# Two-layer hybrid block on one core: expert outputs combined on chip in layer 2, keys as logs in the recurrence

## The chip, the cores and the metric

The kernel runs on one core of a Trainium2 chip. The metric is the device time of one execution in microseconds (us), as the median of several runs. The engines are named as in the profile: PE (TensorE, with PEld for its weight loads), DVE (VectorE), ACT (ScalarE), POOL (GpSimd) and SP (SyncE, which here only issues transfers).

## What is computed

The block has two layers. Each modulates 512 tokens (256 of context, 256 latent) of width 1024, projects them once, runs three token mixers side by side, merges them, and then sends each token through two of 32 experts. The second layer's context is not needed after the mixers, so its mixture of experts sees 256 tokens only.

```python
for layer in range(2):
    hl = xl * (1 + sc1_l) + sh1_l                     # the same for the context tokens
    p = split(hl @ w_in[layer])
    ya, yb, yc = gdn_mixer(p), window_attention_mixer(p), hgrn_mixer(p)
    xl = layer_norm(ALPHA * xl + g1_l * branch_merge(ya, yb, yc, ...))
    h2 = xl * (1 + sc2_l) + sh2_l
    y = hierarchical_moe(h2, ...)                     # top group, two experts in it
    xl = layer_norm(ALPHA * xl + g2_l * y)

# hgrn_mixer: per channel, both directions, chunks of 64
logf = log(max(lb + (1 - lb) * sigmoid(x), 1e-30))
k = (1 - lb) * sigmoid(-x)
b = cumsum(logf)                                      # within the chunk
a[t, s] = sum_d q[t, d] * k[s, d] * exp(b[t, d] - b[s, d])      # s <= t
o = (q * exp(b)) @ S + a @ v
S = exp(b_last) * S + (k * exp(b_last - b)).T @ v

# one expert
hid = silu(xb @ w1[e]) * (xb @ w3[e]);  y = hid @ w2[e]
```

## The kernel before, in words

`backbone` writes both layers out as straight code; a planner orders the instructions of each engine by priority, and `fill` and `bg` set pieces of projection and of modulation work by hand between the steps of the mixers. A conditional block is a unit that nothing is moved across. All transfers of weights are issued by SP in the order written.

**Start.** `mod_prepare` (L215) makes the modulation's inputs, `mod_steps` (L263) multiplies them with the columns of one modulation vector in pieces of 512 KB (L281), and L294 to L303 turn the result into columns. The vectors 0 and 1 come first, then the tokens X are loaded; L424 to L434 transpose X, apply scale and shift (ACT, L432) and split the result into a high and a low part of type fp32r (L433, L434), 256 tokens at a time.

**Projections.** `split_unit` (L140) loads a raw piece of 1024 columns' worth, rounds it to the high part on ACT (L152) and takes the low part on POOL or DVE (L154); `mm3` (L202 to L204) multiplies in three passes. The 17 calls of `init_rows` (background work of the first layer) write X into the two regions of the table `ysD`, so that rows that no expert writes hold numbers.

**HGRN2 (C).** `forget_gates` (L929) makes `kf` (the keys) and `lf` on ACT, POOL and DVE, with L945 the addition of the lower bound in the second layer and L946 the floor; `log_gates` (L948) takes the log of `lf`, 128 channels of both directions at a time (L953). `head_begin` (L1065) makes for each of four heads the cumulative sums `bc` by matmul, the transposed keys `kt` (a copy on ACT), and the decayed keys (`es`, sums at L1087, the product on POOL at L1090). `level_decays` (L1118) subtracts boundary sums into `E` on DVE and takes Exp on ACT; `level_products` (L1137) multiplies the left half of `E` by `kt` on DVE (L1147, two instructions per level and head) and the right half by the queries on POOL, and PE multiplies the two.

**Router (R).** L1481 and L1483 pick the experts on DVE. `permute(q)` (L1542) sorts tokens into expert order by matmul with selection matrices, and copies the sorted rows to `XS` on DVE and ACT. Ahead of `permute(0)` POOL scales a row of norm weights (L1562) and applies scale and shift to X (L1566, 1024 wide, two instructions per block of 128 tokens). Then the token weights are scattered to `wsD` by POOL.

**Experts (E).** `expert_steps` (L1613) computes a block of up to 64 tokens: `weights` loads `wc` from `wsD`, `rows` copies the block's rows (L1634), `up` multiplies with w1 or w3 (L1640, PE in 128 by 64 column tiles, two tiles at a time), `gate` (L1644), `turn` (two transposes and the copy L1651), `down` (L1659, column tiles again), L1663 the weighting, and L1670 two stores of 128 KB to `ysD`. The loop (L1740 to L1765) writes the steps of expert e and e+1 into each other: the first `up` of e+1 stands around `turn` of e, then `down` of e, then the second `up` of e+1. An expert with over 64 tokens runs a conditional block more. An expert's weights are 6 MB in six pieces; the ring of slots holds 18 MB in this loop (15 and `NE2` = 3 slots of 1 MB).

**End.** Four indirect loads gather the rows of `ysD` (L1776), four additions put them to X (L1780), `normalise` ends with L377, then scale, shift and the store of the output.

Of the kernel before, what the change touches and what calls it, by code (L numbers as in the profile page):

```python
# [20 lines left out]
P = 128  # L21
# [60 lines left out]
def backbone(ctx: ExitStack, tc: tile.TileContext, a, out, dbg=None, upto=None):  # L82
# [55 lines left out]
    BOTH = (nc.gpsimd, nc.vector)  # L138

    def split_unit(kt, pieces, engines=(nc.gpsimd,)):  # L140

        n = sum(cn for p in pieces for _, cn in p)
        hr, lr = [wtile(x)[:, :kt * n].bitcast(F32R).rearrange("p (k c) -> p k c", k=kt) for x in ("whi", "wlo")]
        off = 0
        for piece in pieces:
            pn = sum(cn for _, cn in piece)
            rv = rtile()[:, :kt * pn].rearrange("p (k c) -> p k c", k=kt)
            o = 0
            for load, cn in piece:
                load(rv[:, :, o:o + cn])  # L150
                o += cn
# [13 lines left out]
    def cols_unit(src, c0, n, kt=KD, engines=(nc.gpsimd,)):  # L165
        w = 1024 // kt
        return split_unit(kt, [[col_load(src, c, min(w, c0 + n - c))] for c in range(c0, c0 + n, w)], engines)
# [46 lines left out]
    def mod_prepare():  # L214
        with tc.tile_pool(name="modp", bufs=1) as pool:  # L215
            r = pool.tile([2 * NLAYER * KD, P], F32, name="lnr")
            for i, n in enumerate(("ln2_g", "ln2_b")):
                nc.sync.dma_start(r[i * NLAYER * KD:(i + 1) * NLAYER * KD], a[n].rearrange("l (k p) -> (l k) p", p=P))
# [5 lines left out]
            for i, n in enumerate(("ln1_g", "ln1_b")):  # L224
                nc.sync.dma_start(r[2 * NLAYER * i:2 * NLAYER * (i + 1)], a[n].rearrange("l (h c) -> (l h) c", c=512))
            for i in range(NLAYER):
                nc.sync.dma_start(r[4 * NLAYER + 4 * i:4 * NLAYER + 4 * i + 4],
# [21 lines left out]
            for i in range(NLAYER):  # L249
                b = pool.tile([6 * KD, P], F32, name="bm", tag="bm")  # L250
                nc.sync.dma_start(b, a["b_mod"][i].rearrange("(v p) -> v p", p=P))
# [7 lines left out]
                for v in (1, 4):  # L259
                    nc.vector.tensor_scalar(bmT[i][:, v], bmT[i][:, v], 1.0, None, op0=OP.add)  # L260

    def mod_steps(l, v, ahead=0):
# [29 lines left out]
        def finish():  # L292
# [6 lines left out]
            ps = ps_tile([P, 2, P])  # L299
            for x in range(2):  # L300
                transpose(ps[:, x], row[:, x * P:(x + 1) * P])
            for s in range(2):
                nc.vector.tensor_add(modT[l][:, v, s].rearrange("p (j x) -> p x j", x=2),  # L303
                                     ps.rearrange("p x (j m) -> p x j m", m=32)[:, :, :, s],
                                     bmT[l][:, v].rearrange("p (j x) -> p x j", x=2))
# [56 lines left out]
    def normalise(bs):  # L362
# [13 lines left out]
        for i, b in enumerate(bs):  # L376
            nc.vector.tensor_scalar(X[:, b], X[:, b], r[:, i:i + 1], nm[:, i:i + 1], op0=OP.mult, op1=OP.add)  # L377
# [4 lines left out]


    mod_prepare()
    for v in (0, 1):
        for f in mod_steps(0, v):
            f()
# [1426 lines left out]
```

## Time and profile before

| | us |
|---|---|
| median of 3 runs | 2718.26 |
| the three runs | 2717.43, 2718.26, 2724.83 |
| the profiled execution | 2724.99 |
| its span, first to last instruction | 2723.5 |
| PE busy | 2202.1 (81%) |
| DVE busy | 1257.1 (46%) |
| POOL busy | 713.6 (26%) |
| ACT busy | 615.9 (23%) |
| read from and written to HBM | 592.36 and 59.03 MB |
| mean granted clock of PE | 0.907 |

The profiled execution is one program run recorded by the hardware. The shares are means over stages with different limits: a share tells nothing until it is read for one stage. The page cuts the span into 40 equal slices of 68 us; in each, a digit is the busy share of an engine in tenths, and a number the rate at which the transfers moved bytes. From there the stages are read one by one, with windows of the trace (busy time per engine in a stretch), the waits of one engine, and timelines (start, duration, engine, line, operation, and in brackets the idle time before it with what ended that).

### The profile page before, as it was taken

To read this page: it belongs to the slowest core of one execution; us is meant where nothing else is said; L and a number is where in the kernel's file an instruction comes from. 1 tells how busy PE (TensorE), PEld (TensorE's weight loads), DVE (VectorE), ACT (ScalarE), POOL (GpSimd) and SP (SyncE) were. 2 spreads that over 40 slices of the span, in tenths; PEclk is the share of its full clock that TensorE was granted. 3 is DMA by queue.
4 is the path that set the end of the run, shared out by engine and by line. 5 is a ranking of instruction groups with operands and counts; after the bars stand their busy time and mean duration, and the time that the engine had idled before them with its cause. 6 is when DMAs were issued, how large, how long until landed. Compare 5 with 4: busy or idle time off the path is not lost. (4 is left out here: it accounts for less than half of the span.)

```text
span 2723.5 us, 42854 instructions
## 1 busy us (share of the span) xinstructions
PE 2202.1 (81%) x16239; PEld 1554.5 (57%) x16239; DVE 1257.1 (46%) x2596; ACT 615.9 (23%) x1233; POOL 713.6 (26%) x757
## 2 busy tenths in 40 slices
PE   7998988887988889877773899986787669778774
PEld 3665985676776554444441666875777545344432
DVE  4749545787448322212224779457875411111112
ACT  2421335543332000000000342335543200000000
POOL 1242220454244211111112242213554131111111
PEclk9999999898989899888987899988998889998897
DMA  9466351222657469999997258342356949999995
GB/s 319 146 204 201 117 186 47 76 86 89 197 174 248 155 244 361 416 416 416 417 411 247 64 167 258 107 161 62 102 147 191 333 173 383 417 416 417 417 416 217
DMA packets 325669, 655.09 MB, mean 241 GB/s; under 512 B 48662, under 2 KB 228414, under 8 KB 282136
## 3 DMA queue, kind: packets, MB, share of 16 engines
q1 hardware_dynamic: 291058, 600.76, 60.9%
q10 hardware_dynamic: 21382, 26.79, 2.8%
q0 software_dynamic: 12960, 23.94, 2.6%
q8 instruction: 171, 2.80, 0.4%
q14 instruction: 98, 0.80, 0.1%
HBM read 592.36 MB, written 59.03 MB: 239 GB/s over the span
## 5 line engine op out<-in xcount | busy, mean ns | idle before, releaser
L1640 PE MATMUL ps<-we,xt 128*64 128x256 f32 x4224 | 548.4, 412 | 180.3 <-DMA we<-in_w 161.1
L1640 PEld LDWEIGHTS ps<-we,xt 128*64 128x64 f32 x4224 | 330.6, 148 | 389.1 <-issue 262.7
L154 POOL TENSOR_TENSOR wlo<-raw,whi 128x1024 fp32r<-128x1024 f32 (+1 forms) x84 | 206.9, 2464 | 548.7 <-ACT whi L152 508.5
L202 PE MATMUL ps<-hT,whi 128*128 128x512 f32 (+2 forms) x880 | 328.0, 373 | 2.0 <-ACT whi L152 1.9
L204 PE MATMUL ps<-hT,wlo 128*128 128x512 f32 (+2 forms) x880 | 317.9, 361 | 0.3 <-DVE wlo L154 0.3
L203 PE MATMUL ps<-hT,whi 128*128 128x512 f32 (+2 forms) x880 | 317.6, 361 | 0.0
L1659 PE MATMUL ps<-we,hd 128*64 128x512 f32 x1104 | 251.8, 598 | 4.7 <-DVE hd L1651 4.7
L1670 POOL DMA_DIRECT2D ysD<-yo x134 | 71.4, 533 | 698.1 <-DMA ysD<-yo 348.2
L1644 ACT ACTIVATE hd<-ps 128x256 f32<-128x256 f32 x69 | 26.4, 383 | 969.0 <-PE ps L1640 969.0
L152 ACT ACTIVATE whi<-raw 128x1024 fp32r<-128x1024 f32 x174 | 180.0, 1044 | 236.0 <-PE ps L203 130.3
L1663 DVE SCALAR_TENSOR_TENSOR yo<-ps,wc,g 128x512 f32<-128x512 f32 x69 | 51.8, 751 | 374.5 <-PE ps L1659 337.0
L202 PEld LDWEIGHTS ps<-hT,whi 128*128 128x128 f32 (+1 forms) x880 | 172.9, 196 | 43.0 <-issue 13.4
L204 PEld LDWEIGHTS ps<-hT,wlo 128*128 128x128 f32 (+1 forms) x880 | 172.4, 196 | 31.2 <-issue 6.9
L203 PEld LDWEIGHTS ps<-hT,whi 128*128 128x128 f32 (+1 forms) x880 | 173.0, 197 | 25.2 <-issue 3.7
L1651 DVE COPY hd<-ps 128x256 f32<-128x256 f32 x69 | 29.3, 425 | 305.2 <-PE ps L110 305.1
L154 DVE TENSOR_TENSOR wlo<-raw,whi 128x1024 fp32r<-128x1024 f32 x90 | 147.3, 1638 | 45.2 <-ACT whi L152 39.4
L1659 PEld LDWEIGHTS ps<-we,hd 128*64 128x64 f32 x1104 | 78.7, 138 | 135.9 <-issue 120.0
L1627 POOL DMA_DIRECT2D wc<-wsD x138 | 71.7, 520 | 173.2 <-DMA ysD<-yo 71.3
L203 PE MATMUL ps<-wlo,hT 128*128 128x256 f32 x384 | 109.8, 286 | 1.6 <-DVE wlo L154 1.6
L202 PE MATMUL ps<-whi,hT 128*128 128x256 f32 x384 | 110.5, 288 | 0.0
L204 PE MATMUL ps<-whi,hT 128*128 128x256 f32 x384 | 109.4, 285 | 0.0
L281 PE MATMUL ps<-wmod,sT 128*32 128x256 f32 x768 | 88.2, 523 | 10.7 <-DMA wmod<-in_w_mod 6.5
(429 smaller groups left out, 3840.5 us busy)
## 6 DMA issues: line engine op xcount, KB each, us to landing
we<-in_w SPq DMA_DIRECT2D x338, 1024.0 KB
raw<-in_w_in SPq DMA_DIRECT2D x124, 512.0 KB
wmod<-in_w_mod SPq DMA_DIRECT2D x96, 512.0 KB
we<-in_w SPq DMA_DIRECT2D x92, 512.0 KB
ysD<-yo POOLq DMA_DIRECT2D x134, 128.0 KB, 5.7
ysD<-X SPq DMA_DIRECT2D x17, 512.0 KB
raw<-in_w_out SPq DMA_DIRECT2D x16, 512.0 KB
mgD<-st ACTq DMA_DIRECT2D x24, 256.0 KB
```

The lines of the kernel that those rows point to most:

```text
L152: nc.scalar.activation(hr[:, :, off:off + pn], rv, AF.Copy)
L154: eng.tensor_sub(lr[:, :, off:off + pn], rv, hr[:, :, off:off + pn])
L202: mm(ps, st[0](k), mv[0](k), start=(k == 0), stop=False)
L203: mm(ps, st[0](k), mv[1](k), start=False, stop=False)
L204: mm(ps, st[1](k), mv[0](k), start=False, stop=(k == kt - 1))
L281: mm(hold["ps"][32 * j:32 * j + 32, :], sT[:, k, :], cols, start=(k == 0), stop=(k == KD - 1 and v not in mod_d[l]))
L1627: nc.gpsimd.dma_start(tl["wc"][grp[g]], wsD[ds(off, RB)])
L1640: mm(t["ph"][grp[g], i], t["xt"][:, k], (w1, w3)[i](k, g * 256, 256), start=(k == 0), stop=(k == KD - 1), tile_position=(0, g * RB))
L1651: nc.vector.tensor_copy(hh, pt)
L1659: mm(py[grp[g]], hh[:, j, grp[f]], w2(k, g * 512, 512), start=(k == 0), stop=(k == 3), tile_position=(0, g * RB))
L1663: nc.vector.scalar_tensor_tensor(tl["hd" if x else "yo"], py, tl["wc"][:, x:x + 1], g2[x], op0=OP.mult, op1=OP.mult)
L1670: (nc.scalar if last else nc.gpsimd).dma_start(ysD[region, ds(off, RB), g * 512:(g + 1) * 512], tl["yo"][grp[g]])
```

## The change

In words:

- **Layer 2, experts.** The table `ysD`, the table `wsD`, the stores, the loads of `wc` and the gathers are gone. Per expert, DVE multiplies the output by the modulation gate (`gated`), ACT and DVE split it into high and low parts, DVE makes a selection matrix `st` from the tokens' positions, PE multiplies in row tiles (64 partitions deep, 128x512, eight per expert), and DVE adds the result, times the token's weight, to X (four instructions 128x512). These additions (`pending`) are set into the second `up` of the next expert. `rows` masks the rows beyond the expert's count instead of copying. Blocks beyond 64 tokens add in line. `NE2` becomes 1 there. Expert 0's output is kept in `y0` until its positions are laid out.
- **Layer 1, experts.** One region of `ysD` instead of two, without `init_rows`.
- **Router.** Scale and shift of X move from POOL to DVE, behind the selection matrices of `permute(1)`; the row's scaling moves to ACT; the region offsets are gone.
- **HGRN2.** `kf` gets the floor too (four instructions of 128x1024 per layer) and its log (eight more of 128x512). `bk` = `bc` minus the transposed log keys takes the place of the copy `kt`. The products L1147 and L1090 are gone; 32 matmuls with the identity add the log keys in PSUM ahead of Exp. At the last level the keys are transposed again and exponentiated.
- **Start.** The vectors 0 and 1 are loaded together in pieces of 1 MB, with X and four raw pieces of `w_in` between them; X is transposed meanwhile (`XT`); the high and low parts are made 512 tokens wide. Small loads move from SP to ACT's queue.
- **Small moves.** `normalise` at the end of the experts applies its scale on ACT; two units per layer-2 convolution take the low part on POOL.

```diff
-    for v in (0, 1):
-        for f in mod_steps(0, v):
-            f()
+    for k in range(KD):
+        wm[k] = wtile("wmod")
+        nc.sync.dma_start(wm[k], a["w_mod"][0, k * P:(k + 1) * P, 0:2 * D])
+        if k < NB:
+            x_load(k)
+        else:
+            if k < KD - 1:
+                raw_load(k * P)
+            for x in range(2 * (k - NB), 2 * (k - NB) + 2):
+                nc.scalar.activation(XT[:, x], x_T(0, NB, x), AF.Copy)
...
-    background[:0] = [lambda i=i: init_rows(i) for i in range(NR * YROWS // RB // 2)]
...
+        for k in range(KD):
+            xt = x_T(0, NB, k) if l else XT[:, k]
...
+            parts(k, slice(0, T), ht, nc.gpsimd if l and k % 2 else nc.vector)
...
-                nc.vector.tensor_scalar(lf[:, c], lf[:, c], 1e-30, None, op0=OP.max)
+                for x in (lf, kf):
+                    nc.vector.tensor_scalar(x[:, c], x[:, c], 1e-30, None, op0=OP.max)
...
+                    for x in (lf, kf):
+                        lv = x[:, :, d * HID + h * P:d * HID + (h + 1) * P]
...
-                nc.scalar.activation(kt[:, d], ps.rearrange("p c t -> p (c t)"), AF.Copy)
+                nc.vector.tensor_sub(bk[:, d], bc[:, d], ps.rearrange("p c t -> p (c t)"))
...
-                    mm(ps[:, c], (ls, us)[d], lf[:, c, cols[d]], start=True, stop=True)
-                es = ct([P, NB, P], "es")
-                nc.scalar.activation(es, ps, AF.Exp)
-                nc.gpsimd.tensor_mul(kf[:, :, cols[d]], kf[:, :, cols[d]], es)
+                    mm(ps[:, c], (ls, us)[d], lf[:, c, cols[d]], start=True, stop=False)
+                    mm(ps[:, c], ident, kf[:, c, cols[d]], start=False, stop=True)
+                nc.scalar.activation(lf[:, :, cols[d]], ps, AF.Exp)
...
-                nc.gpsimd.tensor_add(E[:, 0, q0:], H["kt"][:, 0, q0:], H["kt"][:, 1, q0:])
+                for d in range(2):
+                    ps = ps_tile([P, NB, P])
+                    for c in blocks:
+                        transpose(ps[:, c], kf[:, c, H["cols"][d]])
+                    nc.scalar.activation(E[:, d, q0:], ps.rearrange("p c t -> p (c t)")[:, q0:], AF.Exp)
...
-                EL = halves(E[:, 0], hb)
-                for s in range(2):
-                    nc.vector.tensor_mul(EL[:, :, s], EL[:, :, s], halves(H["kt"][:, s], hb)[:, :, s])
...
-        nc.gpsimd.tensor_scalar(lnrow, lnrow, ALPHA, None, op0=OP.mult)
-        for b in blocks:
-            for op, x in ((nc.gpsimd.tensor_mul, 0), (nc.gpsimd.tensor_add, 4)):
...
+        def scale_rows(ins):
+            with tc.issue_after(ins):
+                for b in blocks:
+                    for op, x in ((nc.vector.tensor_mul, 0), (nc.vector.tensor_add, 4)):
...
+        def returned(e, first, py, n=1):
+            pool = late["pool"]
+            yo = [gated(py, x) for x in range(nst)]
+            st, sid = [pool.tile([P, w], dt, name=x, tag=f"{x}{n}") for x, w, dt in (("st", nt, F32R), ("sid", 1, F32))]
+            nc.vector.tensor_scalar(sid, row, first, cs_[:, 1, ds(e, 1)], op0=OP.add, op1=OP.add)
+            nc.vector.tensor_scalar(st, late["pos"][:, 0], sid, None, op0=OP.is_equal)
+            nc.vector.scalar_tensor_tensor(st, late["pos"][:, 1], sid, st, op0=OP.is_equal, op1=OP.add)
+            parts = {x: in_parts(yo[x], n) for x in range(nst if n > 1 else 1)}
+            def add(b):
...
+                ps = [ps_tile([P, 512], "pj") for _ in range(2)]
+                for i, y in enumerate(parts[x]):
+                    for g in range(2):
+                        mm(ps[g], st[grp[g], b * P:(b + 1) * P], y[grp[g]], start=(i == 0), stop=(i == 1),
+                           tile_position=(g * RB, 0))
+                for g in range(2):
+                    xv = X[:, b0 + b, g * 512:(g + 1) * 512]
+                    nc.vector.scalar_tensor_tensor(xv, ps[g], wtok[:, b, ds(e, 1)], xv, op0=OP.mult, op1=OP.add)
...
-        NE2 = 3
+        NE2 = 1 if onchip else 3
...
-            up(1, range(KD))
+            for k in range(0, KD, KD // nb):
+                up(1, range(k, k + KD // nb))
+                if onchip:
+                    pending.pop(0)()
```

## Rows read from the trace of the kernel before

**Rows 1.** The page's 40 slices: the rate of all transfers, GB/s in each
```profile
GB/s 319 146 204 201 117 186 47 76 86 89 197 174 248 155 244 361 416 416 416 417 411 247 64 167 258 107 161 62 102 147 191 333 173 383 417 416 417 417 416 217
```

**Rows 2.** Windows: us; busy PE, PEld, DVE, ACT, POOL; clock, DMA share, GB/s
```profile
500.00:665.00 165.00, 131.45 (x1401) 108.92 (x1403) 140.45 (x276) 71.49 (x112) 91.02 (x61) 0.91 0.29 88
...
862.00:885.00 23.00, 12.91 (x66) 4.56 (x65) 22.92 (x39) 5.40 (x15) 22.05 (x9) 0.71 0.53 182
1885.00:2010.00 125.00, 101.43 (x1099) 93.19 (x1100) 100.85 (x282) 59.20 (x107) 67.83 (x64) 0.92 0.36 102
...
2304.00:2683.00 379.00, 296.41 (x1974) 157.06 (x1970) 47.88 (x95) 9.53 (x25) 50.34 (x96) 0.91 1.01 413
```

**Rows 3.** Queue q0, 2304 to 2683 us: packets, MB, share of 16 engines
```profile
q0 software_dynamic: 3952, 6.44, 4.7%
```

**Rows 4.** Waits of PE, 2304 to 2683 us: sum, count, longest
```profile
PE ps L1640 <- DMA we<-in_w: 76.7, 24, 5.3
```

**Rows 5.** Timeline of the start: us, duration, engine, line, operation [idle before]
```profile
33.39 0.42 DVE L294 COPY row<-ps 128x256 f32<-128x256 f32 x1 [11.43 <-PE ps L281]
...
36.60 0.43 DVE L434 TENSOR_TENSOR hT<-ht,hT 128x256 fp32r<-128x256 f32 x1
...
48.26 0.80 PE L204 MATMUL ps<-hT,wlo 128*128 128x512 f32 x1 [0.27 <-DVE wlo L154]
```

**Rows 6.** Windows of L1147 alone, 500:665 and 1885:2010: the closing sum
```profile
sum 290.00, DVE 64.20; mean DVE 32.10
```

**Rows 7.** The same windows of L1087 alone: the closing sum
```profile
sum 290.00, PE 19.11 PEld 18.73; mean PE 9.55 PEld 9.37
```

**Rows 8.** Waits of PE, 500 to 670 us: sum, count, longest
```profile
PE ps L110 <- DVE es L1197: 18.0, 3, 7.0
```

**Rows 9.** Timelines of POOL and DVE in the first router
```profile
865.35 18.78 POOL L1566 TENSOR_TENSOR X<-X,XS 128x1024 f32<-128x1024 f32 x8
...
873.34 1.58 DVE L1483 TENSOR_TENSOR oh<-eq,mxi 128x128 f32<-128x128 f32 x1
...
884.64 0.29 DVE L1483 TENSOR_TENSOR oh<-eq,mxi 128x128 f32<-128x128 f32 x1
```

**Rows 10.** The page's costliest groups: busy, mean ns of one, idle before
```profile
L154 POOL TENSOR_TENSOR wlo<-raw,whi 128x1024 fp32r<-128x1024 f32 (+1 forms) x84 | 206.9, 2464 | 548.7 <-ACT whi L152 508.5
```

**Rows 11.** Timelines of DVE and ACT, the second layer's forget gates
```profile
1843.81 3.31 DVE L945 TENSOR_TENSOR lf<-lf,lbr 128x1024 f32<-128x1024 f32 x1
...
1857.52 0.68 DVE L946 TENSOR_SCALAR lf<-lf 128x1024 f32<-128x1024 f32 x1
...
1880.66 4.27 ACT L953 ACTIVATE lf<-lf 128x512 f32<-128x512 f32 x8
```

**Rows 12.** Timeline from the second router into the experts
```profile
2169.33 3.65 PE L1659 MATMUL ps<-we,hd 128*64 128x512 f32 x16 [0.52 <-DVE hd L1651]
...
2187.61 0.60 ACT L1560 ACTIVATE XS<-ps 128x512 f32<-128x512 f32 x1 [19.81 <-POOL X L1566]
...
2201.52 0.83 PE L1640 MATMUL ps<-we,xt 128*64 128x256 f32 x5 [2.48 <-DVE xt L1634]
```

**Rows 13.** Timeline of PE, one expert whose weights are there
```profile
2210.30 0.50 PE L110 MATMUL ps<-cst,hd 128*128 128x128 f32 x2
...
2210.74 1.95 PE L1640 MATMUL ps<-we,xt 128*64 128x256 f32 x16
...
2212.51 3.60 PE L1659 MATMUL ps<-we,hd 128*64 128x512 f32 x16
...
2215.95 3.62 PE L1640 MATMUL ps<-we,xt 128*64 128x256 f32 x32
```

**Rows 14.** Timeline of DVE at the end
```profile
2688.29 0.75 DVE L1663 SCALAR_TENSOR_TENSOR yo<-ps,wc,g 128x512 f32<-128x512 f32 x1 [3.76 <-PE ps L1659]
...
2707.73 1.21 DVE L1780 TENSOR_TENSOR X<-X,yg 128x1024 f32<-128x1024 f32 x1
```

More of the change, by code (lines that the diff above doesn't have):

```diff
@@ L138, in backbone @@
     BOTH = (nc.gpsimd, nc.vector)
+    early = {}
     def split_unit(kt, pieces, engines=(nc.gpsimd,)):
-        n = sum(cn for p in pieces for _, cn in p)
+        n = sum(x[1] for p in pieces for x in p)
         hr, lr = [wtile(x)[:, :kt * n].bitcast(F32R).rearrange("p (k c) -> p k c", k=kt) for x in ("whi", "wlo")]
@@ L1614, in expert_steps @@
-        def expert_steps(tl, e, off, piece=None, region=None):
+                    if not (k == "xt" and static or onchip and k in ("yo", "wc"))}
+        grp = [slice(g * RB, (g + 1) * RB) for g in range(2)]
+        late = {}
+        def expert_steps(tl, e, off, first, piece=None):
             piece = piece or (lambda j: pieces[6 * e + j])
-            region = e % NR if region is None else region
             w1, w3 = [lambda k, *cols, j=j: piece(j + k // 4)(k % 4, *cols) for j in (0, 2)]
@@ L1669, in down @@
                 for g in range(2):
-                    (nc.scalar if last else nc.gpsimd).dma_start(ysD[region, ds(off, RB), g * 512:(g + 1) * 512],
+                    (nc.scalar if last else nc.gpsimd).dma_start(ysD[ds(off, RB), g * 512:(g + 1) * 512],
                                                                  tl["yo"][grp[g]])
-            return rows, up, gate, turn, down, weights
-        def expert_block(*args):
-            rows, up, gate, turn, down, weights = expert_steps(*args)
-            weights()
+            return rows, up, gate, turn, down
@@ L1678, in expert_block @@
+        def expert_block(tl, e, off, first, piece=None, y=None):
+            rows, up, gate, turn, down = expert_steps(tl, e, off, first, piece)
             rows()
@@ L1682, in expert_block @@
             turn()
-            down()
+            py = down()
+            if y is not None:
+                nc.scalar.activation(y, py, AF.Copy)
+            elif onchip:
+                for add in returned(e, first, py):
+                    add()
         def counted(i, e, top):
@@ L1761, in backbone @@
                 turn()
-            down()
+            py = down()
+            if onchip:
+                pending = returned(e, 0, py, 2)
             with tc.If(cnt > RB, label=f"beyond{l}_{e}", preferred_fallthrough_block=True):
-                expert_block(block_tiles(px, *ZO), e, more(off + RB))
+                expert_block(block_tiles(px, *ZO), e, more(off + RB), RB)
             reload(e)
+        if onchip:
+            for add in pending:
+                add()
         W_.close()
```

314 lines of the change are left out of this document (194 added, 120 removed).

## The prediction

> **What bounds the kernel now.** Read the rate of the transfers over the span first [rows 1]. It stands at 411 to 417 GB/s in two plateaus, slices 17 to 21 and 35 to 39: the expert loops of both layers, some 760 us, are paid in bytes. Everywhere else it is below that, and the engines and their waits set the pace. Then the windows [rows 2]. In the second layer's loop the transfers are busy all the time (share 1.01, 413 GB/s), PE for 296 of 379 us, and PE waits 76.7 us in 24 times for weights [rows 4], 3.2 us per expert. In the first layer's recurrence (500 to 665 us) DVE is busy for 140 of 165 us, PE for 131, POOL for 91: no engine is full, each waits for another in turn, and PE's wait behind DVE's L1197 [rows 8] is 18.0 us in 3 times. In the first router DVE has no gap (22.92 of 23 us) and POOL neither.
>
> **The base.** The profiled execution took 2724.99 us around a span of 2723.5, 6.7 above the median of 2718.26. The terms below come out of the trace, and I take the 6.7 as scatter between runs: the sum is subtracted from 2718.26 (from the profiled execution it would end 6.7 higher). A difference of 0.3%, about 8 us, is what a measurement of this kernel can tell from no change.
>
> **Start: -5 (-10 to +2).** Now the modulation row is copied at 33.39 and PE's stream of projections flows from 48.26 [rows 5], 14.9 us in which tokens are transposed, modulated and split in small pieces. Afterwards X is transposed while the weights load, and what is left per 128 channels is modulation on ACT and a cast and a subtraction on DVE, 512 wide. A subtraction of 256 columns takes 0.43 [rows 5], so twice that, and somewhat less for the cast: about 1.4 per channel block, 8 of them, 11 us paced by DVE, with PE beginning on the first. Against that 1 MB more is asked for ahead of the projections, some 3 us at 319 GB/s [rows 1]. If loads stay the limit there, the gain is nil.
>
> **HGRN2, first layer: -6 (-15 to +5).** Removed: L1147 on DVE, 64.2 us over both layers [rows 6], about 32 per layer (the longer stage has more of it), and POOL's product. Added: eight subtractions out of PSUM, priced by the 0.68 to 1.21 of a 128x1024 pass [rows 11, 14] at some 0.7 each, 5.6 us; 32 matmuls with the identity and four more sets of transposes on PE, nearest row L1087 with 9.55 us per layer [rows 7], so about 11; and per layer four floors of 0.68 and eight logs of 4.27 / 8 = 0.53 [rows 11]. DVE falls from 140 to about 112 busy, PE rises from 131 to 142 of 165 [rows 2]. So the 33 idle us of PE can shrink by some part of the 26 that DVE gains, but PE's own 11 are on the path: I take half of PE's idle time, -17, plus 11. The other ends: PE alone sets the end with its stalls unchanged (+5, its work partly in old gaps), or the stage ends at 142 plus 8 of stalls (-15). The logs and floors before it cost 2 to 5 on ACT, already in these numbers.
>
> **Router, first layer: -9 (-13 to -4).** POOL's scaling runs from 865.35 for 18.78 us, and beside it a DVE operation with two inputs of 128x128 takes 1.58, where behind it the same takes 0.29 [rows 9]. Eight operations are slowed by 1.3 to 2.0, 13.5 us together, in a stretch in which DVE has no gap [rows 2]. Moving the scaling behind the selection matrices frees these; the scaling then costs DVE eight passes of 1.21 [rows 14] beside the first experts, where DVE is idle. What limits the gain is the modulation work of POOL and PE set there by hand. The four fewer scatter sources and the missing region offsets go in here; removing the 17 `init_rows` gives nothing, since they lie in a stage whose transfers are at about 150 to 200 GB/s [rows 1] of the 417 possible.
>
> **Between the layers: -2 (-8 to +5).** Four applications of the norm leave DVE (under 1 us each), and four low parts go to POOL at 2.46 each [rows 10]. POOL work beside DVE is what slowed DVE above, so the two may cancel.
>
> **Mixers, second layer: +2 (-6 to +10).** The same recurrence with fewer rows: PE 101 of 125, DVE 101 [rows 2], so PE's extra 9 meet 24 of idle time and the relief is smaller. And the forget gates there are the chain that PE waits for: DVE's addition takes 3.31 beside POOL [rows 11]; four more floors of 0.68 (as much as four times that beside POOL) and 4.27 us more of logs stand ahead of the copies that follow on ACT.
>
> **Router and experts, second layer: -10 (-24 to +20).** Three things. First, expert 0 is done on PE at 2169.33 + 3.65 = 2172.98, and expert 1 starts at 2201.52, since the copies of sorted rows on ACT wait 19.81 us for POOL's scaling [rows 12]. Without POOL in that chain I put the start at 2186 to 2188, 14 to 16 earlier, after the position rows and the masks. The loads that refill the ring start as much earlier. Second, the ring has two slots less, 2 MB, 5 us at 413 GB/s. Third, the small transfers: POOL's queue holds 4.7% of the transfer engines' time [rows 3], 17.8 of 379 us, 0.74 per expert, and the cadence of 15.8 us per expert (379 / 24) falls to about 15.1. That only comes if PE keeps below it. PE needs for an expert 2 x 3.62 + 0.44 + 3.60 = 11.3 [rows 13]. Added are eight matmuls of 128x512 at 3.60 / 16 = 0.23, 1.8, and stalls where the addition waits for DVE's multiply (0.75 [rows 14]), ACT's high part and DVE's low part while the first half of `up` takes only 1.8: some 0.6. So 13.8, with 13 (pairs side by side) and 14.8 as ends. Two experts have over 64 tokens and pay an addition in line, 4 to 6 us each, which eats the margin: from about 14.8 on, each 0.5 us per expert costs 31 x 0.5 = 15.5 us. At 13.8 the three come to -11 to -14, at 14.5 to -7, at 15 to +6; I take -10.
>
> The rule that speaks against this: the loop switches between column tiles and row tiles four times more per expert. In the trace two transposes over the whole array, between column-tiled stretches, take 2210.74 - 2210.30 = 0.44 [rows 13]; were all of it the two changes of form, four changes more would cost 0.9 per expert, an expert would take 14.7, and the loop's term would be about -2. The Trainium skill (TensorEngine Tiling (Array Packing), Key Properties) says that changing the tiling mode drains TensorE. By that rule the 0.9 is to be added, and the sum would be -35, 2683; the row is an upper bound for it, since the transposes themselves are in the 0.44, so I leave it out of the sum and in the range. No run here shows the row-tiled form yet.
>
> **End: -13.5 (-15 to -11).** The weighting starts at 2688.29, and the last addition of gathered rows ends at 2707.73 + 1.21 = 2708.94 [rows 14]: store, its landing, four gathers and additions, 20.7 us. After: multiply 0.75, high and low part about 0.6 and 0.7, matmuls, four additions of 0.75, together about 7.
>
> **Sum.** -5 - 6 - 9 - 2 + 2 - 10 - 13.5 = -43.5, so 2718.26 - 43.5 = 2674.8, predicted **2675**.
>
> **Rivals.**
> - PE takes over the second layer's loop, chance 0.08, the slower side. If the additions run at half the clock (eight of 0.45, 3.6) and wait 0.7 for their parts at both places, an expert takes 11.3 + 3.6 + 1.4 = 16.3. Against: PE's granted clock is 0.91 in the loop [rows 2]; busier PE may lower it. It decides from 16.1 us per expert: there the loop's term is +41 in place of -10, the total +8, 2726 and more.
> - The stores' time was hidden anyway, chance 0.14: weights alone hold the loop at its cadence because bytes, not queue time, are the limit (413 GB/s against 417 elsewhere [rows 1, 2]). Then 15 of the 17.8 us don't come: 2690.
> - The logs cost PE what they give DVE, chance 0.12: both recurrences end by PE, +5 and +10 in place of -6 and +2, and the between-layers term +3: 2699.
> - More comes, chance 0.10: PE's stalls in the recurrence go (-15), the additions go in pairs, the router's full 13: 2645 to 2656.
> - Forecast, chance 0.56: 2656 to 2688.
>
> That the change does not do what it says would need POOL's scaling or the stores to be still there; it can't be from the diff, only the order by priorities can shift work, which the ends of each term hold.
>
> **How the numbers follow.** Faster by over 0.3%: 0.56 + 0.14 + 0.10 and 0.08 of the 0.12 = 0.88; within 0.3%: 0.04, from the third rival's upper part; slower: 0.08, the first. The range of 8 in 10 reaches from 2645 to 2708: it leaves out the first rival and the outer parts of the third and fourth, about 0.17.
>
> **What would show it.** Right: in the second loop no POOL transfers, the cadence at 15.1 to 15.3 and PE still waiting for weights about 1 us per expert; PE's expert 1 at 2186 to 2188 less what came before it; the last addition 7 us after the last product; in the first router DVE's 128x128 operations at 0.29 throughout; in the first recurrence PE's busy time up by 11 and its idle time down by more. Wrong: PE without waits in the second loop and a cadence over 15.8; the first recurrence longer than 165 us with PE full; the forget gates of the second layer later by more than 10.

## Result

The changed kernel takes 2675.09 us (median of 4 runs, 2673.15 to 2684.13) against 2717.85 before (4 runs, 2716.07 to 2724.83): a ratio of 0.9844 with a 95% interval of 0.9816 to 0.9873. The forecast was 2675, range 2645 to 2708. The profiled executions stand as the medians do: 2724.99 before, 2684.13 after, 40.9 us apart. The number was met in good part by luck: misses of 5 to 13 us cancel. Two terms came out much better or worse than put down, and two gains that were put down were not there. The rest of this part is about those.

The profile after, the page's engine shares (busy us, share of the span, instructions): POOL has lost 143 us, PE and DVE have gained 62 and 97.

```profile
PE 2264.1 (84%) x16695; PEld 1583.1 (59%) x16695; DVE 1353.8 (50%) x2787; ACT 659.4 (25%) x1302; POOL 570.7 (21%) x578
```

Windows of the changed kernel to set against [rows 2] (columns as there): the first recurrence from its first to its last product, the first router up to its first selection product, and the second layer's loop over as long a stretch as in [rows 2].

```profile
515.50:670.60 155.10, 149.29 (x1630) 124.84 (x1631) 101.03 (x218) 71.01 (x110) 74.85 (x58) 0.96 0.31 93
838.00:870.00 32.00, 25.86 (x185) 13.25 (x182) 19.30 (x80) 12.33 (x29) 0.30 (x1) 0.84 0.77 237
2263.00:2642.00 379.00, 357.47 (x2292) 177.55 (x2288) 169.81 (x332) 26.40 (x52) 0.00 (x0) 1.00 1.01 414
```

In the recurrence PE is now busy for all but 6 of 155 us; in the loop PE is at 357 of 379, DVE at 170 instead of 48, POOL at nothing, and the transfers still have a share of 1.01: that loop is still paid in bytes, at a shorter cadence (time from one expert to the next).

To see where the time went, I take the start of the same instruction (the n-th product of the same source line) in both traces. The differences of such starts scatter: two executions of the changed kernel (the run "again" below) lie up to 9 us apart at a boundary and 2 at the end. So only the length of a stage within one trace is read, and a few us of it mean little.

| stage, from start to start | before | after | again | forecast of its change | measured |
|---|---|---|---|---|---|
| to the first projection product | 46.8 | 45.6 | 45.9 | | |
| to the first product with the first DeltaNet's state | 300.7 | 303.3 | 299.3 | -5 | 0 |
| first recurrence, first to last product | 172.0 | 156.4 | 153.1 | -6 | -16 to -19 |
| first router to expert loop's last product | 606.9 | 599.6 | 602.3 | -9 | -5 to -7 |
| from there to the first product of the second layer's DeltaNet gates | 104.9 | 111.0 | 113.8 | -2 | +6 to +9 |
| second HGRN2's forget gates (ACT) to its recurrence's first product | 64.9 | 72.0 | 70.6 | } +2 | +6 to +7 |
| second recurrence | 112.8 | 107.7 | 109.1 | } | -4 to -5 |
| second router to the loop's last product | 547.4 | 538.9 | 539.9 | -10 | -8 |
| end | 35.8 | 21.3 | 21.3 | -13.5 | -14.5 |

The rows add up to some -35 and -36, of 40.9 and 43.1 between the traces; the rest lies in stages for which nothing was forecast, and is no more than the scatter.

How far a length scatters is seen from the traces of all kernels below whose edit leaves that stage as it is: 150.0 to 157.0 for the first recurrence (172.0 before), 593.5 to 602.3 for the first router and expert loop, 111.0 to 118.8 for the passage between the layers (up to 115.7 but for one), 536.9 to 542.1 for the second router and loop. Of the kernel before there is one trace. A difference of a length counts here when it lies outside these ranges.

### The profile page after: what moved, and what is told of

Same layout as the page of the kernel before. It is cut to its first block, busy times and chain, and to the rows that moved or that the text cites. A ratio compares the mean times of both kernels' runs of the same rounds, so it can differ in the third digit from the quotient of the medians.

```text
span 2682.6 us, 43323 instructions
## 1 busy us (share of the span) xinstructions
PE 2264.1 (84%) x16695; PEld 1583.1 (59%) x16695; DVE 1353.8 (50%) x2787; ACT 659.4 (25%) x1302; POOL 570.7 (21%) x578
## 5 line engine op out<-in xcount | busy, mean ns | idle before, releaser
L1706 PE MATMUL ps<-we,xt 128*64 128x256 f32 x4288 | 574.6, 399 | 120.8 <-DMA we<-in_w 100.5
L157 POOL TENSOR_TENSOR wlo<-raw,whi 128x1024 fp32r<-128x1024 f32 (+1 forms) x88 | 218.0, 2479 | 571.9 <-ACT whi L155 517.2
L205 PE MATMUL ps<-hT,whi 128*128 128x512 f32 (+2 forms) x880 | 323.1, 368 | 2.7 <-DVE st L489 2.7
L206 PE MATMUL ps<-hT,whi 128*128 128x512 f32 (+2 forms) x880 | 314.6, 358 | 0.7 <-POOL hT L458 0.6
L157 DVE TENSOR_TENSOR wlo<-raw,whi 128x1024 fp32r<-128x1024 f32 x86 | 136.9, 1592 | 60.6 <-ACT whi L155 53.4
L1731 DVE SCALAR_TENSOR_TENSOR yo<-ps,wc,g 128x512 f32<-128x512 f32 x35 | 26.3, 751 | 177.3 <-PE ps L1725 172.0
L1778 DVE SCALAR_TENSOR_TENSOR X<-ps,wr,X 128x512 f32<-128x512 f32 x136 | 95.4, 745 | 38.6 <-PE ps L1774 38.5
L1738 POOL DMA_DIRECT2D ysD<-yo x68 | 36.4, 535 | 367.6 <-DMA ysD<-yo 186.0
L1746 DVE TENSOR_TENSOR yo<-ps,g 128x512 f32<-128x512 f32 x33 | 22.8, 692 | 161.0 <-PE ps L1725 161.0
```

The source lines that it names most:

```text
L157: eng.tensor_sub(lr[:, :, off:off + pn], rv, hr[:, :, off:off + pn])
L205: mm(ps, st[0](k), mv[0](k), start=(k == 0), stop=False)
L206: mm(ps, st[0](k), mv[1](k), start=False, stop=False)
L1706: mm(t["ph"][grp[g], i], t["xt"][:, k], (w1, w3)[i](k, g * 256, 256), start=(k == 0), stop=(k == KD - 1), tile_position=(0, g * RB))
L1731: nc.vector.scalar_tensor_tensor(tl["hd" if x else "yo"], py, tl["wc"][:, x:x + 1], g2[x], op0=OP.mult, op1=OP.mult)
L1738: (nc.scalar if last else nc.gpsimd).dma_start(ysD[ds(off, RB), g * 512:(g + 1) * 512], tl["yo"][grp[g]])
```

## Experiments

Each undoes one part of the change, changes one size, or doubles one cost. Their kernels run in three groups, each on one chip with its own runs of the kernel before (2724.03, 2723.11 and 2727.55); what is compared across groups is the ratio to those. With the intervals of two such ratios their difference is known to some 9 to 11 us; what is smaller than that is not shown by the times, and only a stage's length can tell it.

**The base, once more.**

> The changed kernel once more, as the base for the runs that undo a part of it: 2675, within 8 us. A trace of its own tells which stage boundaries repeat from one execution to the next: if the stages are the cause, each boundary lies within 2 us of that of the first trace; if the differences between traces are scatter, they move by 5 and more.

2679.16, ratio 0.9822 (0.9799 to 0.9846). The boundaries moved by more than 2 us (by 8.8 at the first router), so differences between traces of single boundaries are not evidence by themselves; the lengths of stages in the table repeat within 1 to 4 us in these two traces, over all traces within 5 to 9.

**The recurrence with linear keys.**

> The changed kernel with the recurrence as before (linear keys, the products on DVE and POOL). Theory of the forecast: the logs give -6 in the first layer and cost 2 in the second, so 4 us slower than the changed kernel. Rival, read from the landmarks of the two traces (boundary shifts of -16.8 from 380 to 680 us and -2 from 1775 to 2128): the logs were worth three times as much, so 14 to 19 us slower, with PE's waits behind DVE's copy of es back at about 18 us in the first layer.

```diff
-                nc.vector.tensor_sub(bk[:, d], bc[:, d], ps.rearrange("p c t -> p (c t)"))
+                nc.scalar.activation(kt[:, d], ps.rearrange("p c t -> p (c t)"), AF.Copy)
...
-                    mm(ps[:, c], (ls, us)[d], lf[:, c, cols[d]], start=True, stop=False)
-                    mm(ps[:, c], ident, kf[:, c, cols[d]], start=False, stop=True)
-                nc.scalar.activation(lf[:, :, cols[d]], ps, AF.Exp)
+                    mm(ps[:, c], (ls, us)[d], lf[:, c, cols[d]], start=True, stop=True)
+                es = ct([P, NB, P], "es")
+                nc.scalar.activation(es, ps, AF.Exp)
+                nc.gpsimd.tensor_mul(kf[:, :, cols[d]], kf[:, :, cols[d]], es)
...
+                EL = halves(E[:, 0], hb)
+                for s in range(2):
+                    nc.vector.tensor_mul(EL[:, :, s], EL[:, :, s], halves(H["kt"][:, s], hb)[:, :, s])
```

2695.84, ratio 0.9897 (0.9875 to 0.9919): 17 us slower than the base, on the same chip. The rival was right, the forecast's 4 was not. Its first recurrence takes 172.0 us, as before the change. In the second layer forget gates and recurrence together take 179.3 us, as with the logs (179.7 and 179.6): 6.5 less for the gates, 6.1 more for the recurrence. The waits of PE in the first recurrence (sum, count, longest), first with linear keys, then in the changed kernel:

```profile
PE ps L110 <- DVE es L1233: 17.7, 3, 7.0
PE ps L1196 <- DVE E L1183: 6.3, 4, 2.0
PE ps L1196 <- POOL E L1180: 4.6, 3, 1.9
```
```profile
PE ps L110 <- DVE es L1236: 5.8, 2, 3.5
PE ps L1191 <- POOL E L1186: 3.1, 1, 3.1
```

And the window of the recurrence with linear keys, from its first to its last product:

```profile
508.00:679.00 171.00, 142.37 (x1539) 117.95 (x1540) 138.70 (x268) 68.46 (x107) 91.43 (x64) 0.91 0.28 83
```

The wait behind DVE's es, which stood in [rows 8] with 18.0, falls to 5.8, and that behind the DVE products (6.3) is gone. The run undoes the products on DVE, the one on POOL and the logs all at once; that DVE's relief is what counted is read from these waits, no run takes it alone.

**The start as before.**

> The changed kernel with the start as before (vectors 0 and 1 one after the other, then X, transposes after them, pieces of 256 tokens). Theory of the forecast: 5 us slower. Rival: the first layer's DeltaNet is paced by a DVE chain that ends where it ended before, whatever the projections do, and the earlier loads only move the wait: within 3 us of the changed kernel, and the boundary at 300 us in the trace moves by less than 3.

```diff
-        nc.sync.dma_start(wm[k], a["w_mod"][0, k * P:(k + 1) * P, 0:2 * D])
...
+    for v in (0, 1):
+        for f in mod_steps(0, v):
+            f()
+    for b in range(NB):
+        x_load(b)
```

2681.34, ratio 0.983 (0.9805 to 0.9855): not told apart from the base. The first product with the DeltaNet's state comes at 303.3 in its trace, 303.3 with the new start. The timeline of the changed kernel's start shows why:

```profile
37.56 1.93 PE L421 MATMUL ps<-wmod,sT 128*32 128x256 f32 x16 [2.29 <-DMA wmod<-in_w_mod]
...
38.71 0.42 DVE L425 COPY row<-ps 128x256 f32<-128x256 f32 x1 [5.70 <-PE ps L421]
...
40.91 0.41 DVE L425 COPY row<-ps 128x256 f32<-128x256 f32 x1
...
45.63 1.22 PE L205 MATMUL ps<-hT,whi 128*128 128x512 f32 x2
```

The second of the two modulation rows, which all else waits for, is copied at 40.91, where it was at 33.39 [rows 5]: its weights now share the transfers with X and three raw pieces (the fourth follows them). From that row to the first product it is 4.7 us instead of 13.4 (46.8 in the table less 33.39), so the part on chip has indeed become shorter, and the loads took it back.

**The passage between the layers as before.**

> The changed kernel with the passage between the layers as before (the norm applied on DVE, the low parts of two units on DVE, transposes in pieces of 256 tokens in the second layer). Theory of the forecast: 2 us slower. Rival: the landmarks lose 4 us from 1590 to 1700, in the second layer's DeltaNet, so the POOL low parts cost more than they free: 4 us faster than the changed kernel, with that loss gone.

```diff
-            normalise([b0 + b, b0 + b + 1], nc.scalar)
+            normalise([b0 + b, b0 + b + 1])
...
-(nc.gpsimd,) if j >= 8 or l and j in (4, 6) else (nc.vector,), l)
+(nc.gpsimd,) if j >= 8 else (nc.vector,), l)
```
(and the transposes of the second layer in pieces of 256 tokens again)

2671.04, ratio 0.9797 (0.9775 to 0.9819): 8 us faster than the changed kernel on the same chip, which the times alone don't settle. From the first loop's last product to the second layer's gates it takes 105.0, as before the change (104.9), where the kernels with the new passage take 111.0 to 118.8. By this length the loss is real, though it lies before the place that the expectation named: in the passage, not in the DeltaNet behind it.

**Only the low parts back on DVE.**

> The changed kernel with one line undone: the low parts of two units of the second layer's projection on DVE again; the norm stays on ACT and the pieces 512 wide. If POOL's work beside DVE's additions is the cause of what the passage between the layers lost (an addition took 2.76 us beside it in the trace, 1.21 alone): 6 to 8 us faster than the changed kernel, as with all three edits undone. If the cause is the norm on ACT or the wider pieces: no change.

```diff
-(nc.gpsimd,) if j >= 8 or l and j in (4, 6) else (nc.vector,), l)
+(nc.gpsimd,) if j >= 8 else (nc.vector,), l)
```

2672.69, ratio 0.9795 (0.9773 to 0.9817): 6 to 7 us faster, as much as all three edits undone within what can be told apart; the passage takes 107.1. The timelines show the mechanism. First the changed kernel (POOL, then DVE), then this one:

```profile
1462.30 12.41 POOL L157 TENSOR_TENSOR wlo<-raw,whi 128x1024 fp32r<-128x1024 f32 x4
...
1461.50 1.17 DVE L1924 TENSOR_TENSOR X<-X,yg 128x1024 f32<-128x1024 f32 x1
...
1463.19 2.76 DVE L1924 TENSOR_TENSOR X<-X,yg 128x1024 f32<-128x1024 f32 x1
```
```profile
1449.10 2.40 DVE L1924 TENSOR_TENSOR X<-X,yg 128x1024 f32<-128x1024 f32 x2
```

POOL's four low parts take 12.41 us, and each DVE addition that falls beside them 2.76 instead of 1.20; three of these and a small operation of 2.30 lie in the chain that PE waits for. PE's wait for the norm is 41.9 us in the changed kernel and 37.7 here.

**POOL's scaling back in its place.**

> The changed kernel with the scaling of X back on POOL, ahead of the first selection matrices, in both layers. Theory of the forecast: the first router loses its 9 us, and in the second layer expert 1 starts about 8 later, of which the loop hides the part in which it waits for weights anyway: 9 to 15 us slower. Rival: the modulation work set there by hand hid it: under 4 us slower.

```diff
-        nc.scalar.activation(lnrow, lnrow, AF.Copy, scale=ALPHA)
...
+        nc.gpsimd.tensor_scalar(lnrow, lnrow, ALPHA, None, op0=OP.mult)
+        for b in blocks:
+            for op, x in ((nc.gpsimd.tensor_mul, 0), (nc.gpsimd.tensor_add, 4)):
+                xv = X[:, b].rearrange("p (k c) -> p k c", c=QT)
+                op(xv, xv, lnrow[:, x:x + 4])
...
-                scale_rows(ins)
```

2693.21, ratio 0.988 (0.9852 to 0.9909), some 15 us slower by the ratios; its profiled execution is 7.8 longer than that of the base. The size was as forecast, the place was not. In the first router the selection products begin 40.1 us after the router's first product, as before (40.0), and 31.4 in the changed kernel: the 9 us are there, and DVE's operations on 128x128, 1.58 beside POOL and 0.29 without it [rows 9], take 0.28 there. But by the down products of expert 0's second block (it has over 64 tokens) the two are level, 77.4 and 77.8 after the router's first. First that operation on DVE and PE's timeline in expert 0 in the changed kernel, then this one:

```profile
854.00 0.28 DVE L1541 TENSOR_TENSOR oh<-eq,mxi 128x128 f32<-128x128 f32 x1
...
886.30 7.13 PE L1706 MATMUL ps<-we,XS 128*64 128x256 f32 x64 [0.94 <-DVE X L1643]
900.33 0.70 PE L110 MATMUL ps<-cst,hd 128*128 128x128 f32 x2 [6.91 <-DVE hd L1711]
901.55 5.76 PE L1725 MATMUL ps<-we,hd 128*64 128x512 f32 x16 [0.52 <-DVE hd L1717]
```
```profile
887.29 7.13 PE L1710 MATMUL ps<-we,XS 128*64 128x256 f32 x64 [0.93 <-DVE modT L270]
895.35 0.51 PE L110 MATMUL ps<-cst,hd 128*128 128x128 f32 x2 [0.93 <-DVE hd L1715]
896.37 3.65 PE L1729 MATMUL ps<-we,hd 128*64 128x512 f32 x16 [0.52 <-DVE hd L1721]
...
907.87 0.51 PE L110 MATMUL ps<-cst,hd 128*128 128x128 f32 x2 [0.94 <-DVE hd L1715]
908.89 3.65 PE L1729 MATMUL ps<-we,hd 128*64 128x512 f32 x16 [0.52 <-DVE hd L1721]
```

In the changed kernel PE waits 6.91 us for expert 0's gate, and the 16 products behind the wait take 5.76 instead of 3.65 (granted clock 0.59 from 900.3 to 907.1, mostly the lower of its two levels, 1.2 GHz; 1.00, the upper, in the products ahead of the wait). DVE's eight passes over X are the smaller part of that wait: they end at 894.36, some 1 us behind the products of `up`. The larger part is what stands between them and the gate on DVE, one more selection matrix, for which DVE waits 3.81 us on POOL (L1605, behind the scatters of the token weights):

```profile
898.56 0.48 DVE L1606 SCALAR_TENSOR_TENSOR on<-io,posq,on 128x256 fp32r<-128x256 f32 x1 [3.81 <-POOL on L1605]
899.86 0.42 DVE L1711 TENSOR_TENSOR hd<-hd,ps 128x256 f32<-128x256 f32 x1 [0.81 <-DVE on L1606]
```

In the second layer the trace shows 4 to 5 us more from the router to expert 0 and 1 to 2 more in the loop. The passage between the layers, which the edit doesn't touch, is 118.8 in it, the longest of all. Where the remaining part of the 15 us of the medians lies is not shown by this one trace.

**The scaling behind expert 0.**

> The changed kernel with the first layer's scaling of X a quarter later, behind the selection matrices of permute 2, so that it stands behind expert 0 on DVE. If what DVE's scaling costs is expert 0's wait (its product waited 6.91 us for DVE in the trace): expert 0 takes 9 us in place of 15 to 18 and the first loop ends 3 to 7 us earlier. If the loads pace that loop from its start: expert 0 is earlier, the loop's end and the time are the same.

```diff
-            if q == 1:
+            if q == max(1, nqt - 2):
                 scale_rows(ins)
```

2679.33, ratio 0.9823 (0.9805 to 0.9842): the time of the changed kernel. Expert 0 is nearly as short as with POOL (10.6 us from its first product to its down product, against 9.1 with POOL and 15.2 and 17.7 in the two traces of the changed kernel), so the wait is due to where the scaling stands. The stage ends 592.9 us after the router's first product, in the two kernels of the last experiment, which share the edit, 591.8 and 594.8. The nine traces with the scaling as in the changed kernel have 593.5 to 602.3, 598.7 in the mean: some 5 us, of which a part may be scatter. That the gain doesn't show in the time leaves open whether it is given back later.

**The second layer's experts through memory.**

> The changed kernel with the second layer's experts through memory as the first layer's (one region, ring of 18 slots). Theory of the forecast: the end is 13.5 longer, the loop's transfers get back 0.74 us per expert, 17 to 23 in all, and the two slots more give 5 back: 25 to 31 us slower, cadence 15.7 to 16 in the loop. Rival (the stores' time is hidden): 8 to 14 us slower, cadence as in the changed kernel, 15.0.

```diff
-        onchip = not need_ctx
+        onchip = False
```

2684.68, ratio 0.9845 (0.9815 to 0.9875): by the ratios about 6 us slower than the base, which is not told apart from none, by the trace 19 within the stage (loop 5.4, end 13.8). Both are below the 25 to 31 of the forecast's terms. The cadence over the last 18 steps of the loop (its very last left out) is 16.0 us in this kernel and 15.3 in the changed one (15.8 and 15.3 in the pair that ends this section), so in that part 0.5 to 0.7 of the stores' 0.74 per expert does come free, and the rival that calls it hidden falls for that part.

**Two slots less in the ring.**

> The changed kernel with two slots of 1 MB less in the ring of the second layer (14 in place of 16). Theory of the forecast: 2 MB less are loaded ahead, 5 us slower. Rival: the loads stand still between 2162 and 2262 us because the slots come free an expert at a time, so a smaller ring makes every expert wait and costs over 10 us; or the loop is far enough from its bound that it costs nothing.

```diff
-        NEW = 6 if need_ctx else 9
+        NEW = 6 if need_ctx else 7
```

2684.29, ratio 0.9844 (0.9813 to 0.9875), 6 us above the base by the ratios, which is within their scatter; from the second router to the loop's last product 547 us instead of 537 to 542. So by this one trace 2 MB ahead are worth 5 to 10; that it is more than the 5 that the bytes take is not shown. The transfers are not busy early in the loop in either kernel (272 GB/s from 2140 to 2304 us here, 259 in the changed kernel, 416 and 417 later); that they wait for slots, which come free an expert at a time, is argued from the order of the loads.

**The additions' products twice.**

> The changed kernel with each of the eight matmuls of an expert's addition issued twice into the same place. In the trace of the changed kernel PE takes 14.08 us per expert where weights are there, and the loads 15.0. Eight more matmuls cost 1.0 to 1.9 us. If PE becomes the bound at about 15 us, as the forecast's slower rival has it: an expert takes 15.1 to 16.0, the loop grows by 8 to 35 us, and PE no longer waits for weights. If the loads keep the bound: under 4 us slower.

```diff
-                for i, y in enumerate(parts[x]):
+                for i, y in [*enumerate(parts[x])] * 2:
```

2698.79, ratio 0.99 (0.9869 to 0.9931): 21 us slower. PE no longer waits for weights at all, and where weights are there an expert takes 15.0 us instead of 14.08. So PE is the bound from about 15 us on, and the changed kernel stands 0.9 us per expert below that. PE's timeline: a pair of products (one on each half of the array), two products of `up`, three pairs in a row, and the next column-tiled stretch:

```profile
2324.23 0.51 PE L1774 MATMUL ps<-yh,st 64*128 64x512 f32 x2
2324.66 0.65 PE L1706 MATMUL ps<-we,xt 128*64 128x256 f32 x2
2325.24 0.50 PE L1774 MATMUL ps<-yl,st 64*128 64x512 f32 x2
2325.58 0.39 PE L1774 MATMUL ps<-yh,st 64*128 64x512 f32 x2
2325.80 0.40 PE L1774 MATMUL ps<-yl,st 64*128 64x512 f32 x2
2326.13 1.94 PE L1706 MATMUL ps<-we,xt 128*64 128x256 f32 x14
```

Inside a row-tiled stretch a pair starts 0.22 after the pair ahead of it (2325.58 to 2325.80). A single product of 512 columns on the whole array starts 0.23 after the one ahead of it in the projections of the changed kernel, so the two halves run side by side: eight products more cost 0.9, not 1.8.

**A better version, and what the on-chip half is worth in it.**

> The changed kernel with the passage between the layers as before and the first layer's scaling behind expert 0. If both gains hold and add: 10 to 14 us faster than the changed kernel. If the first loop's loads swallow the second: 7 to 9 faster.

> The same with the second layer's experts through memory: what the on-chip half is worth, on one chip with its base. By the sum of the forecast's terms (end 13.5, transfers 17 to 23, ring -5): 25 to 31 us slower than the kernel with it. By the first trace of that half undone (end 13.8, loop 5.4): 17 to 21 us slower. By the medians of that run: 4 to 10 us slower.

The first is the changed kernel with the edits of "the passage as before" and "the scaling behind expert 0", the second sets `onchip = False` in it. They take 2671.64, ratio 0.9783 (0.976 to 0.9807), and 2683.97, ratio 0.9849 (0.9825 to 0.9872). The first beats the changed kernel by 8 to 11 us; it is not told apart from "only the low parts back on DVE", so nothing beyond the passage's gain is shown. Against it the path through memory costs 12 us by the medians on the same chip: by the traces 14.2 at the end and 1 in the loop. The waits of PE and the POOL queue from 2304 to 2600 us with the memory path:

```profile
PE ps L1710 <- DMA we<-in_w: 66.5, 23, 4.8
```
```profile
q0 software_dynamic: 3028, 5.00, 4.6%
```

## Why the prediction was right, and where its steps failed

**The start** (forecast -5, measured 0). The step failed that counts the wait after the row alone. From the second row to the first product it went from 13.4 to 4.7 us (the forecast's 14.9 runs to a product of the third pass), more than put down, but the row itself comes 7.5 later. The forecast named this end ("if loads stay the limit there, the gain is nil") and took the other value.

**HGRN2, first layer** (forecast -6, measured -16 to -19). The mechanism fits the waits, the step "I take half of PE's idle time" was mis-sized. Against the run with linear keys DVE falls by 38 us over the stage (138.70 to 101.03), PE's own work rises by 7 (142.37 to 149.29; 11 was put down), and PE's idle time went from 29 us to 6, not to 17. The waits [rows 8] could have been followed by name: 18.0 behind es, and the waits behind L1147 on top, all end on DVE, so DVE's relief had a claim on all of them. PE's work grew by less than the instructions alone would have it, while the granted clock of the stage stands at 0.96 instead of 0.91; the two belong together in the rows, which is cause isn't shown.

**Router, first layer** (forecast -9, measured -5 to -7, and not by the step). The 8.6 to 8.8 us at the selection products came as put down. The step that failed is the one that costs the scaling at nothing "beside the first experts, where DVE is idle": the new order there puts expert 0's gate, which DVE must do, behind the passes and a selection matrix that waits for POOL, and PE waits 6.91 us. With POOL's scaling the stage is as short (597.4). What shortens it against the kernel before in all the kernels run, by 5 to 15 us, is something that they share, and the traces show where. In the kernel before, DVE's weighting of expert 0's first block waits for the token weights, which are loaded behind the scatters; the gate of the second block needs the buffer `hd` of that weighting, and PE waits for the gate:

```profile
928.81 0.75 DVE L1663 SCALAR_TENSOR_TENSOR yo<-ps,wc,g 128x512 f32<-128x512 f32 x1 [12.25 <-DMA wc<-wsD]
...
933.21 0.70 PE L110 MATMUL ps<-cst,hd 128*128 128x128 f32 x2 [6.04 <-DVE hd L1645]
934.43 6.41 PE L1659 MATMUL ps<-we,hd 128*64 128x512 f32 x16 [0.52 <-DVE hd L1651]
```

That wait is 0.94 in the changed kernel and with POOL's scaling, and the products behind it take 3.65 there: 5.1 and 2.8 us less. With POOL's scaling expert 1 starts 107.4 us after the router's first product instead of 115.3, which is these 7.9. Counted from the same product, the scatters start 4 us earlier there and the token weights land 5 earlier. Which edit does that (the change does without the region offsets, among others) no run separates.

**Between the layers** (forecast -2, measured +6 to +9). The forecast said that POOL beside DVE may cancel the gain, from [rows 9], and did not carry the price through: 2.76 against 1.20 for an addition of X is of the kind of [rows 11] (3.31 beside POOL for a pass that takes 1.21 without it [rows 14]), and these additions were on the chain that PE waits for. The same row that priced the gain in the router should have priced the loss here.

**Mixers, second layer** (forecast +2, measured +2). Forget gates to recurrence +7, recurrence -5; the run with linear keys has the two together as long as the changed kernel, so the logs cost nothing here; the 2 us are not theirs, and they lie within the scatter (175.0 to 180.0 over the kernels with logs). The first transpose of the attention weights, which DVE finishes behind the forget gates, waits 19.67 us (17.22 before), and ACT's copies behind the logs hold PE for another 6.07, where PE has no such wait before:

```profile
1850.32 1.94 PE L110 MATMUL ps<-cst,p 128*128 128x128 f32 x8 [19.67 <-DVE p L1041]
...
1875.60 2.45 PE L1060 MATMUL ps<-pT,vtok 128*64 128x128 f32 x16 [6.07 <-ACT pT L1051]
```

**Router and experts, second layer** (forecast -10, measured -8). The -10 stands on no sum: the parts as written (-14 to -16, +5, -17.8 and 8 to 12 for additions in line) come to -15 to -21, not to the "-11 to -14" at 13.8 us, so that it came close is luck. The three parts: expert 1 starts 8.3 us after expert 0's products end instead of 28.5, 20 earlier; expert 0 itself comes 3.7 later behind the router, so 16 to 17 are left (14 to 16 were put down):

```profile
2155.05 3.65 PE L1725 MATMUL ps<-we,hd 128*64 128x512 f32 x16 [0.56 <-issue]
...
2167.02 5.40 PE L1706 MATMUL ps<-we,xt 128*64 128x256 f32 x48 [1.50 <-DMA we<-in_w]
```

The transfers' share came, but only over the last 18 steps, in which the loads are the bound in both kernels: the cadence goes there from 15.9 to 15.3, some 10 us, not 17.8. And an expert whose weights are there takes 14.08 us of PE, near the 13.8 forecast, instead of 11.5; over the first 13 that, with the two slots, eats most of it. So the on-chip half is worth its end, about 14, and 1 to 5 in the loop. The gain of the stage against the kernel before is mostly POOL's scaling leaving the router (with POOL's scaling back the stage takes 545.1). PE still waits for weights, 1 us a time; the waits of PE from 2263 to 2642:

```profile
PE ps L1706 <- DMA we<-in_w: 10.6, 11, 2.0
PE ps L1706 <- DVE xt L1692: 3.6, 1, 3.6
```

The rule on tiling modes, which spoke against the change: PE's timeline for one expert in the changed kernel is

```profile
2308.12 0.49 PE L1774 MATMUL ps<-yh,st 64*128 64x512 f32 x2
2308.55 0.65 PE L1706 MATMUL ps<-we,xt 128*64 128x256 f32 x2
2309.12 0.49 PE L1774 MATMUL ps<-yl,st 64*128 64x512 f32 x2
2309.55 1.94 PE L1706 MATMUL ps<-we,xt 128*64 128x256 f32 x14
2311.42 0.50 PE L1774 MATMUL ps<-yh,st 64*128 64x512 f32 x2
2311.76 0.40 PE L1774 MATMUL ps<-yl,st 64*128 64x512 f32 x2
2312.09 1.95 PE L1706 MATMUL ps<-we,xt 128*64 128x256 f32 x16
```

An expert goes into row tiles three times, not twice: a pair, a pair and two pairs, which take 0.43, 0.43 and 0.67 us from start to next start. Of these 0.22 per pair are their own, so going into row tiles and back costs 0.21 to 0.23, about 0.11 per change of form, and some 0.65 per expert for six changes. The sum had nothing for it, and the range 0.9 for four. The 14.08 come near the 13.8 because the four pairs take 0.9 where 1.8 were put down. The Trainium skill (TensorEngine Tiling (Array Packing), Key Properties) says that a change of the tiling mode drains TensorE; the trace agrees, at about half of the bound of 0.22 for each that was left in the range.

**The end** (forecast -13.5, measured -14.5). DVE's multiply to the last addition takes 5.5 us where 7 were put down:

```profile
2661.92 0.69 DVE L1746 TENSOR_TENSOR yo<-ps,g 128x512 f32<-128x512 f32 x1 [2.98 <-PE ps L1725]
...
2664.66 2.73 DVE L1778 SCALAR_TENSOR_TENSOR X<-ps,wr,X 128x512 f32<-128x512 f32 x4 [0.59 <-PE ps L1774]
```

**The slower rival.** It was to decide from 16.1 us per expert. With the products doubled PE takes 15.0 and the kernel loses 21 us against the changed one, more than the forecast's scale has (from -10 to +6 at 15), yet it is still 1% faster than before; 16.1 itself was not run. What it feared of the clock didn't happen: the granted clock of the loop is 1.00 (the upper of its two levels, 2.4 GHz, nearly throughout; a lower mean is a mix with 1.2) where PE is busy for 357 of 379 us, and 0.91 before [rows 2] and on the memory path, where PE waits for weights some 23 times.

**What stays open.** Which edit brings the first layer's token weights earlier; where the remaining half of the 15 us lies that POOL's scaling costs by the medians; whether the scaling behind expert 0 is worth anything.

## What to carry to other kernels

Price the relief of an engine by the waits that name it, summed, and not by a share of idle time: where most waits of the busiest engine ended on one other engine, most of them went. Work that is moved carries its price along: look up what the engine must do next at the new place, what that waits for in turn, and what it slows beside it, with the same rows that priced the gain. In a loop that is paid in bytes, a saving per step counts only for the steps in which the loads are the bound; before that, a faster consumer and the depth of the ring count.

## What the runs showed of the hardware

The granted clock rose with the change: 0.91 to 1.00 in the second layer's loop and 0.91 to 0.96 in the first recurrence, both where PE's waits became fewer and shorter. Row-tiled products on the two halves of the array run side by side, a pair in 0.22 us. A DVE addition of two 128x1024 operands takes 2.76 us beside a POOL subtraction and 1.20 alone, and the POOL subtraction 3.1 (12.41 / 4) where the mean over the kernel before is 2.46 [rows 10]: each slows the other. Behind a wait of 6.91 us in expert 0 the same 16 products of PE took 5.76 us at a granted clock of 0.59, and 3.65 without it.
